# One layer of a hybrid RWKV-7 / S5 decoder: S5's merge for both token halves from one weight load and ahead of the RWKV merge, the block inversion issued step by step, and half-array low-rank products

## The chip, the cores and the metric

The program runs on one core of one Trainium2 chip, as a single launch over 1024 tokens of width 1024 in float32. The metric is device time in microseconds (us) from launch to end. The engines are named as in the profile: PE (TensorE) multiplies matrices, PEld is its weight load, DVE (VectorE) and ACT (ScalarE) do elementwise work, POOL (GpSimd) does little but issue transfers, and SP (SyncE) issues most of them. A difference of about half a per cent is what a measurement of this kernel can tell from none.

## The reference

```python
h = rms_norm(x, norm_mix_pre)
proj = h @ w_in                       # r,k,v, three low-rank downs | S5 input u | two gates
o_rwkv = rwkv7_branch(p_rwkv, ...) @ w_branch_rwkv
o_s5   = s5_branch(u_s5, ...) @ w_branch_s5
mixed  = (g_rwkv * o_rwkv + g_s5 * o_s5) @ w_out
x = x + rms_norm(mixed, norm_mix_post)
x = x + rms_norm(conv_ffn(rms_norm(x, norm_ffn_pre), ...), norm_ffn_post)

# inside rwkv7_branch (decay, in-context rate and gate are low-rank, ranks 64, 64 and 128)
w = -softplus(-(w0 + tanh(wd) @ w2)) - 0.5
a = sigmoid(a0 + ad @ a2)
g = sigmoid(gd) @ g2
# inside s5_branch
y = gelu(Re(C s) + D u)
return y * sigmoid(y @ w_glu + b_glu)
```

The RWKV state is carried through 1024 tokens, 8 heads of 64; the S5 state is a diagonal complex recurrence, 32 groups of 64 states. Everything else is dense products.

## The kernel before, in words

**Products.** Activations lie transposed: 128 channels on the partitions, tokens along the row, and the 1024 tokens are cut into two halves of 512, called `th` 0 and 1. Every float32 operand is split into a rounded high part (`hh`, `wh`: an ACT copy, lines 156 and 226) and the rest (`hl`, `wl`: a DVE subtract, lines 157 and 227). `mm3_steps` (lines 172 to 174) multiplies high by high, high by low and low by high: three matmuls of 128x128 by 128x512 for each 128 rows of the contraction. `load_w` fetches a weight tile of 128x512 and splits it. A tile's results collect in a PSUM buffer `gm` and are then evicted by ACT or DVE.

**Order.** The PE's order of instructions is the order in which the program issues them. `drive` in turn advances *lanes* (generators for the S5 scan, for its tables, for RWKV's preparation, chain and output), and between their steps the *fill*: a list of generators of dense products. A lane's `yield (cost, wait)` says what its step costs the PE in planned microseconds and how long the next step is to be held back; in the meantime fill is issued, and `PACE` says how much fill has to be issued per unit of lane work. The constants `T_...` are those waits. They do not make a chip wait: they only decide what stands ahead of what in the order. On DVE and ACT the order is made from priorities and planned readiness; `high_priority(HPW)` puts an instruction ahead of others that are ready.

**Stages of the first half of the program.** First `start` normalises and projects S5's input. Then the S5 stage runs the scan of four batches with `mix_in` as fill: the projections of r, k, v (`rkv`) and the low-rank products (`lowrank`), whose right-hand sides come from input-projection tiles 12 and 13. Then comes RWKV for half 0 and half 1. For each half:

1. `rwkv_front` builds the masked Gram blocks `gr` (lines 660 to 731);
2. `rwkv_inv` inverts the 32x32 diagonal blocks by 30 elimination steps of two DVE instructions each (lines 795 and 797), between two transposes (784, 798) and copies in and out of `gr` (`diagonal`, line 773);
3. `rwkv_level` joins 32-blocks to 64-blocks (line 812 transposes on DVE, 822 and 832 multiply on the PE);
4. `rwkv_chain` runs 8 chunks, each with three short PE steps that wait for ACT and DVE in turn (lines 879 to 904);
5. `rwkv_out` normalises each head, adds the bonus and applies the gate (lines 918 to 951).

The fill beside it is `rkv(2)`, `rkv(3)`, then 16 tiles of gates (`gate_tiles`, evicted at line 1158), then, once half 0 is out, `merge` (half 0: RWKV branch times gate, S5's GLU, S5 branch times gate, sum), `merge_s5` (half 1: GLU and S5 branch) and `outproj(0)`. After RWKV is done, `merge_rk` and `outproj(1)` finish half 1, and the feed-forward part follows, which takes the second half of the span and is not touched.

In the merges, `s5_y` (line 1178) loads the S5 output and applies gelu, `glu_tile` multiplies by `w_glu` and evicts at line 1188, `gate` multiplies by a branch weight and evicts on DVE at line 1203, line 1249 adds the two branches and lines 231 and 232 split the half-scaled sum. Both halves of S5's part load all 12 of its weight tiles (4 of `w_glu`, 8 of `w_br`), each half for itself.

**Low-rank products.** The two rank-64 products (decay and in-context rate) use a weight tile of 128 rows of which 64 are zeros, and one common right-hand side: 2 products by 2 halves by 4 tiles by 3 matmuls.

Of the kernel before, what the change touches and what calls it, by code (L numbers as in the profile page):

```python
# [66 lines left out]
class Kern:  # L67
# [425 lines left out]
    def s5_tables(self, b, d):  # L493
# [70 lines left out]
        for t, f in ((ph, s["fh"]), (sn, s["fl"])):  # L564
            for g in range(8):
                A.activation(t[:, g], self.cst("nrow"), AF.Identity, scale=f[:, b * 8 + g:b * 8 + g + 1])
        V.tensor_scalar(cs, ph, MAGIC, -MAGIC, ALU.add, ALU.add)
# [72 lines left out]
    def rwkv_front(self, d, g, th, pt, start):  # L640
# [122 lines left out]
    def diagonal(self, ds, m, back):  # L763
# [3 lines left out]
        for g, d in enumerate(ds):  # L767
            for blk in range(2):
                for h in range(2):
                    o, q = 64 * h + 32 * blk, 32 * (2 * g + blk)  # L770
                    x = d["gr"][o:o + 32, :, :, h, 32 * blk:32 * blk + 32].rearrange("p u c t -> p (u c) t")
                    y = m[q:q + 32, :, h]
                    (self.nc.scalar.copy if n % 2 else self.nc.vector.tensor_copy)(*((x, y) if back else (y, x)))
                    n += 1

    def rwkv_inv(self, ds, th):
# [5 lines left out]
        with self.tc.high_priority(HPW):  # L782
            self.diagonal(ds, x, False)
# [5 lines left out]
        yield 2.0, 0  # L789
        with self.tc.high_priority(HPW):  # L790
            for q in range(1, 31):
                m = 31 - q
                tm = self.tg("tm", 1, (128, 256), pool=self.rka)
                tv = tm[:, :q * m].rearrange("p (s t) -> p s t", t=m)
                V.tensor_tensor(tv, x2[:, 0:q, q:q + 1].to_broadcast([128, q, m]),
                                m2[:, q:q + 1, q + 1:32].to_broadcast([128, q, m]), ALU.mult)
                V.tensor_tensor(x2[:, 0:q, q + 1:32], x2[:, 0:q, q + 1:32], tv, ALU.add)
            V.transpose(mt.rearrange("p (e t) -> p t e", t=32), x.rearrange("p (q t) -> p t q", t=32))
            self.diagonal(ds, mt, True)

    def rwkv_level(self, ds):
# [13 lines left out]
        yield 0.4, T_LT  # L815
# [45 lines left out]
    def rwkv_chain(self, ds, pt, th):  # L861
# [7 lines left out]
        for c in range(8):  # L869
            z = self.z.pop(c)  # L870
            if th and not self.fac and len(self.ys5) == 4:
# [39 lines left out]
    def rwkv_out(self, ds, th, latency):  # L911
# [3 lines left out]
        for g in range(2):  # L915
# [12 lines left out]
            V.tensor_tensor(yn, yn, y.unsqueeze(2).to_broadcast([128, 16, 64]), ALU.mult)  # L928
        yield 0, latency
        for g, d in enumerate(ds):  # L930
            for u in range(2):
                p = 2 * g + u
                ps = self.rp((128, 4, 128))
                for c in range(4):
                    nc.tensor.transpose(ps[:, c], self.yn[:, g, c, u], self.cst("ident"))
                y1 = self.tg("ld", NLD)
                A.activation(y1, ps.rearrange("p c t -> p (c t)"), AF.Identity, bias=self.vec("lnx_b", p),
                             scale=self.vec("lnx_w", p))
                for src, op in ((d["bv"][u], ALU.add), (self.TG[p][:, o], ALU.mult)):
                    if th:  # L940
                        t = self.fac.pop(0)
                    else:
                        t = self.tg("ld", NLD)
                        nc.sync.dma_start(t, src)
                    V.tensor_tensor(y1, y1, t, op)
# [8 lines left out]
    def inproj(self, *jobs):  # L954

        ws = [self.load_w(self.a["w_in"][mt]) for mt, _ in jobs]
        for th in range(2):
# [133 lines left out]
    def shifted_into(self, xs, mt):  # L1091
# [3 lines left out]
        def use(th, ps):  # L1095
            y = self.shifted(ps, mt, th)
            if mt == 12:
                nc.scalar.activation(y[0:64], y[0:64], AF.Tanh)
            else:
# [5 lines left out]

    def lowrank(self, xs, js):

        nc = self.nc
        for j, hb, dst in js:
            w = self.load_w(self.a["w_lr"][j])  # L1110
            for th in range(2):
                for p in range(4):
# [3 lines left out]
                    if hb is None:  # L1116
                        nc.scalar.copy(t, ps)
                    else:
                        nc.scalar.activation(t, ps, AF.Tanh, bias=self.hb[hb][:, p:p + 1], scale=0.5)
                    if dst is self.TZ:  # L1120
                        nc.scalar.activation(t, t, AF.Identity, bias=self.ones1, scale=1.0)
# [11 lines left out]
    def mix_in(self):  # L1133

        def mixed(a, b, n):

            for i, c in enumerate(a):
                yield c
                if i % n == n - 1:
# [5 lines left out]
        xs = [[], []]  # L1145
# [3 lines left out]
        yield from mixed(self.rkv(1), self.lowrank(xs[1], ((2, None, self.TG),)), 4)  # L1149
# [4 lines left out]
    def gate_tiles(self, *ms):  # L1154
# [5 lines left out]
        yield from self.inproj(*((18 + m, lambda th, ps, m=m: use(m, th, ps)) for m in ms))  # L1160
# [14 lines left out]
    def s5_y(self, t, b, th, y):  # L1175

        self.nc.sync.dma_start(t, self.YU[b].rearrange("j c g n -> (c g) j n")[:, :, th * 64:th * 64 + 64])
        self.nc.scalar.activation(y.rearrange("p (n j) -> p j n", j=8), t, AF.Gelu_apprx_tanh)
        return y

    def glu_tile(self, m, xs, t, y, br, to):

        nc = self.nc
        w = self.load_w(self.a["w_glu"][m])
        ps = self.gmp()
        yield from self.mm3_steps(ps, w, 0, [x[0] for x in xs], [x[1] for x in xs])
        nc.scalar.activation(t, ps, AF.Tanh, bias=self.hb["b_glu"][:, m:m + 1], scale=0.5)
        nc.vector.scalar_tensor_tensor(t, t, 1.0, y(), ALU.add, ALU.mult)
        br.append(to())
        self.split_half(*br[-1], t)  # L1190
# [14 lines left out]
    def merge_load(self):  # L1205

        if self.outs >= 2 and not self.yr:
            for k in range(4):
                self.yr.append(self.tg("ld", NLD))
                self.nc.sync.dma_start(self.yr[k], self.YR[k])  # L1210

# [795 lines left out]
```

## Time and profile before

| | |
|---|---|
| median of three runs | 1464.04 us (1458.7 to 1464.59) |
| the profiled execution | 1461.26 us, its span 1459.5 us |
| PE busy | 1402.2 us, 96% of the span, 9156 matmuls |
| DVE busy | 1087.5 us, 75% |
| ACT busy | 746.7 us, 51% |
| mean granted PE clock | 0.986 |

A matmul's busy time in the profile is longer than the time after which the next one can start, since they overlap; so 96% is not the share of the PE's peak that is used. The windows view gives, for a stretch of the span, each engine's busy time (with the number of instructions), the granted PE clock, the DMA engines' busy share and the rate that they moved. The waits view names the waiting instruction, the one that it waited for, and then the total, the number of waits and the longest, in us.

### The profile page before, as it was taken

The page shows a single profiled execution, that of the slowest core. Times are in us where ns is not written, and L with a number is a line of the kernel's source. Part 1 is how long each engine was busy: PE and PEld are TensorE (multiplying, and loading weights), DVE is VectorE, ACT ScalarE, POOL GpSimd, SP SyncE. Part 2 cuts the span into 40 slices and gives each one's busy share as a digit, 9 for nine tenths or more (in the row PEclk, how much of TensorE's full clock was granted, in tenths as well). Part 3 has the DMA queues.
Part 4 walks back from the last instruction along what each step waited for, and adds up shares of the span by engine and source line. Part 5 has one row for each costly group of instructions (what it writes and reads, how often), then busy time and mean ns, then how long its engine had stood idle before and what let it go on. Part 6 is the DMA issues. An engine that isn't in the chain of part 4 may idle for free. (4 is left out here: it accounts for less than half of the span.)

```text
span 1459.5 us, 23887 instructions
## 1 busy us (share of the span) xinstructions
PE 1402.2 (96%) x9156; PEld 1142.9 (78%) x9156; DVE 1087.5 (75%) x1783; ACT 746.7 (51%) x1197; POOL 34.9 (2%) x80
## 2 busy tenths in 40 slices
PE   7999999999999989899999999999999999999996
PEld 5778888878878767678788887888888887888785
DVE  8986886378327788548688898777777777597677
ACT  7667775453424564535455464454544445444451
POOL 0000000000000000000000000000000000000001
PEclk9999999999999999899999999999999999999998
DMA  7454433542413565433555543222222228934723
GB/s 221 116 190 128 144 117 108 188 146 80 139 60 110 162 193 165 138 111 116 172 195 180 158 133 122 87 83 76 75 84 87 87 73 273 328 112 144 239 79 115
DMA packets 119682, 202.04 MB, mean 138 GB/s; under 512 B 28672, under 2 KB 34944, under 8 KB 119568
## 3 DMA queue, kind: packets, MB, share of 16 engines
q1 hardware_dynamic: 113296, 182.43, 39.4%
q0 software_dynamic: 4544, 15.80, 2.9%
q10 hardware_dynamic: 1728, 2.29, 0.4%
q8 instruction: 72, 1.18, 0.3%
q14 instruction: 42, 0.34, 0.1%
HBM read 148.04 MB, written 50.33 MB: 136 GB/s over the span
## 5 line engine op out<-in xcount | busy, mean ns | idle before, releaser
L172 PE MATMUL gm<-hh,wh 128*128 128x512 f32 x672 | 276.2, 411 | 9.1 <-DVE hl L1203 4.6
L173 PE MATMUL gm<-hl,wh 128*128 128x512 f32 x672 | 264.8, 394 | 0.0
L174 PE MATMUL gm<-hh,wl 128*128 128x512 f32 x672 | 264.6, 394 | 0.0
L156 ACT CAST wh<-wf 128x512 fp32r<-128x512 f32 x171 | 105.2, 618 | 140.9 <-PE gm L173 72.5
L157 DVE TENSOR_TENSOR wl<-wf,wh 128x512 fp32r<-128x512 f32 x171 | 117.2, 688 | 76.2 <-ACT wh L156 75.6
L172 PEld LDWEIGHTS gm<-hh,wh 128*128 128x128 f32 x672 | 127.5, 190 | 41.5 <-DVE hl L1203 5.7
L174 PEld LDWEIGHTS gm<-hh,wl 128*128 128x128 f32 x672 | 127.7, 190 | 27.8
L173 PEld LDWEIGHTS gm<-hl,wh 128*128 128x128 f32 x672 | 127.8, 190 | 24.7 <-issue 1.0
L1626 PE MATMUL d<-xl,wh 128*128 128x512 f32 x308 | 120.7, 392 | 2.1 <-DVE xl L227 2.0
L1625 PE MATMUL d<-xh,wh 128*128 128x512 f32 x308 | 120.8, 392 | 2.1 <-ACT xh L226 2.1
L1627 PE MATMUL d<-xh,wl 128*128 128x512 f32 x308 | 120.6, 392 | 0.0
L1451 PE MATMUL rp<-t,h 128*128 128x512 f32 x216 | 84.4, 391 | 1.5 <-ACT p L1465 1.5
L1453 PE MATMUL rp<-t,l 128*128 128x512 f32 x216 | 84.2, 390 | 0.5 <-DVE l L227 0.5
L1452 PE MATMUL rp<-t,h 128*128 128x512 f32 x216 | 84.1, 389 | 0.0
L1626 PEld LDWEIGHTS d<-xl,wh 128*128 128x128 f32 x308 | 58.2, 189 | 15.5 <-DVE xl L227 3.4
L1625 PEld LDWEIGHTS d<-xh,wh 128*128 128x128 f32 x308 | 58.2, 189 | 14.6 <-ACT xh L226 2.4
L1627 PEld LDWEIGHTS d<-xh,wl 128*128 128x128 f32 x308 | 58.1, 189 | 12.0
L226 ACT CAST h<-r 128x1024 fp32r<-128x1024 f32 x34 | 35.8, 1054 | 61.1 <-PE rp L1452 29.6
L227 DVE TENSOR_TENSOR l<-r,h 128x1024 fp32r<-128x1024 f32 x34 | 41.6, 1225 | 29.2 <-ACT h L226 27.7
L1472 DVE SCALAR_TENSOR_TENSOR y<-zv,vecs,y 128x1023 f32<-128x1023 f32 (+1 forms) x36 | 46.1, 1281 | 8.5 <-ACT y L1470 8.5
L1465 ACT COPY p<-rp 128x512 f32<-128x512 f32 x54 | 31.0, 574 | 36.6 <-PE rp L1453 36.6
L1451 PEld LDWEIGHTS rp<-t,h 128*128 128x128 f32 x216 | 40.5, 188 | 11.1 <-ACT p L1465 2.4
(459 smaller groups left out, 3127.6 us busy)
## 6 DMA issues: line engine op xcount, KB each, us to landing
r<-in_w_up_dram SPq DMA_DIRECT2D x36, 512.0 KB, 3.6
wf<-in_w_in_dram SPq DMA_DIRECT2D x62, 256.0 KB, 3.0
st<-in_w_down_dram SPq DMA_DIRECT2D x55, 256.0 KB, 4.0
st<-ACT SPq DMA_DIRECT2D x44, 256.0 KB, 4.3
wf<-in_w_up_dram SPq DMA_DIRECT2D x36, 256.0 KB, 2.9
ACT<-y POOLq DMA_DIRECT2D x18, 512.0 KB, 2.9
GT<-ev SPq DMA_DIRECT2D x32, 256.0 KB, 2.5
wf<-in_w_br_dram SPq DMA_DIRECT2D x32, 256.0 KB, 2.6
```

What stands on the lines that cost most here:

```text
L156: nc.scalar.copy(h[:, :n], f[:, :n])
L157: nc.vector.tensor_tensor(l[:, :n], f[:, :n], h[:, :n].bitcast(F32), ALU.subtract)
L172: mm(ps, a, xh[k], start=k == 0, stop=False)
L173: mm(ps, a, xl[k], start=False, stop=False)
L174: mm(ps, b, xh[k], start=False, stop=k == n - 1)
L1451: mm(ps, wh[:, c], xh, start=first and k == 0, stop=False, skip_group_check=True)
L1452: mm(ps, wh[:, c], xl, start=False, stop=False, skip_group_check=True)
L1453: mm(ps, wl[:, c], xh, start=False, stop=k == 3, skip_group_check=True)
L1472: V.scalar_tensor_tensor(y[:, lag:], z[:, 0:1024 - lag], self.vec(nme, i), y[:, lag:], ALU.mult, ALU.add)
L1625: mm(ps, wh[:, c], xh[:, x], start=start, stop=False, skip_group_check=True)
L1626: mm(ps, wh[:, c], xl[:, x], start=False, stop=False, skip_group_check=True)
L1627: mm(ps, wl[:, c], xh[:, x], start=False, stop=stop, skip_group_check=True)
```

## The change

The S5 part of the merge becomes one generator, `s5_unit`, for both halves: each of its 12 weight tiles is loaded once and used for both. It stands in the fill behind the last gate tiles and no longer depends on RWKV's half 0. Gelu moves beside the S5 scan: `s5_ready` applies it after each batch and stores the result in a new DRAM tensor `Y5`, from where `s5_unit` loads it. The merge of half 0 is what is left, `merge_rk0`; it and `outproj(0)` are all the fill that is added when half 0 is out. The last two gate tiles take half 1 first.

The inversion's 60 instructions are no longer issued in one go: after each step the lane yields until `begin + pace * q`, the pairs keep their order in the program on DVE, and the copies back are issued in four portions.

The two rank-64 products use 64-row slices for their third term: the high parts of both weights sit with the low parts of the same weight in one 128-row tile, so that one full matmul gives high by high and low by high, and a 64-row matmul gives high by low. They begin 12 steps into the projection of k, r, v.

Smaller edits: loads of RWKV's operands for half 0 go to POOL's queue, the factors of `rwkv_out` for half 0 are loaded a little earlier, the phase activations of the S5 tables are issued in four portions, and the planned waits and `PACE` have new values.

```diff
@@ rwkv_front
-            nc.sync.dma_start(t, src[:, o])
+            (nc.sync if th else nc.gpsimd).dma_start(t, src[:, o])
@@ rwkv_inv
+        begin, pace = self.now, T_Q2 if th else T_Q
+        for q in range(1, 31):
...
+            with self.tc.high_priority(HPW):
+                c = V.tensor_tensor(tv, x2[:, 0:q, q:q + 1].to_broadcast([128, q, m]),
+                                    m2[:, q:q + 1, q + 1:32].to_broadcast([128, q, m]), ALU.mult)
+                self.tc.keep_in_program_order(c)
+                c = V.tensor_tensor(x2[:, 0:q, q + 1:32], x2[:, 0:q, q + 1:32], tv, ALU.add)
+                self.tc.keep_in_program_order(c)
+            yield 0, begin + pace * q - self.now
@@ low-rank
+    def lowrank_pair(self, w, xs, js):
...
+                ps = [self.gmp() for a in range(2)]
+                for a in range(2):
+                    mm(ps[a], w[a][:, o], hi[a], start=True, stop=False)
+                for a, sl in enumerate(HALF):
+                    mm(ps[a], w[a][sl, o], lo[sl], start=False, stop=True)
+                yield 0.7
@@ mix_in
-        yield from mixed(self.rkv(0), self.lowrank(xs[0], ((0, "w0", self.TZ), (1, "a0", self.TA))), 3)
+        rkv = self.rkv(0)
+        yield next(rkv)
+        w = self.lowrank_w(js)
+        yield from mixed(rkv, self.lowrank_pair(w, xs[0], js), 4, 12)
@@ S5's merge
+    def s5_ready(self, b, tile=None):
+        for th in range(2):
+            t, y = tile(), tile()
+            self.nc.gpsimd.dma_start(...)      # YU[b] -> t
+            self.nc.scalar.activation(..., AF.Gelu_apprx_tanh)
+            self.nc.gpsimd.dma_start(self.Y5[b][:, th * 512:th * 512 + 512], y)
+    def s5_unit(self):
+        xs = [[self.halved(self.pair(1, 4 * th + b), self.Y5[b][:, o[th]]) for b in range(4)] for th in range(2)]
+        br = ([], [])
+        for m in range(4):
+            w = self.load_w(self.a["w_glu"][m])
+            for th in range(2):
...
+                nc.gpsimd.dma_start(y[1].bitcast(F32), self.Y5[m][:, o[th]])
+                yield from self.mm3_steps(ps, w, 0, [x[0] for x in xs[th]], [x[1] for x in xs[th]])
...
+        for m, th in [(m, th) for m in range(6) for th in range(2)] + [(6, 1), (7, 1), (6, 0), (7, 0)]:
+            if m not in ws:
+                ws[m] = self.load_w(self.a["w_br"][1, m])
...
+            yield from self.mm3_steps(ps, ws[m], 0, [x[0] for x in br[th]], [x[1] for x in br[th]])
+            nc.vector.scalar_tensor_tensor(f, t, 1.0, ps, ALU.add, ALU.mult)
+            if (m, th) == (7, 1):
+                self.yr_loads()
@@ the fill
-                self.fill = [self.mix_in()] + [self.gate_tiles(m) for m in range(14)] + [
-                    self.merge_loads(), self.gate_tiles(14, 15)]
+                self.fill = [self.mix_in()] + [self.gate_tiles(0)] + [self.s5_last()] + [self.gate_tiles(m) for m in range(1, 14)] + [
+                    self.gate_tiles(14, 15, order=(1, 0)), self.s5_unit()]
...
-                self.fill += [self.merge(mg), self.merge_s5(self.first), self.outproj(0, mg, self.mx0)]
+                self.fill += [self.merge_rk0(mg), self.outproj(0, mg, self.mx0)]
@@ planned waits
-T_LD, T_SQ, T_LT = 6.0, 3.0, 3.5
+T_LD, T_SQ, T_LT, T_LT2 = 12.86, 3.76, 4.74, 1.89
-T_LN, T_LE, T_INV2 = 32.0, 16.0, 46.0
+T_LN, T_LE, T_INV2 = 50.1, 14.13, 1.95
+T_Q, T_Q2 = 0.66, 1.2
+T_BACK, T_DIAG, T_PH = 3.0, 0.59, 0.41
-PACE, CREDIT = 0.8, 2.0
+PACE, CREDIT = 0.89, 2.0
```

More of the change, by code (lines that the diff above doesn't have):

```diff
@@ L935, in rwkv_out @@
                     nc.tensor.transpose(ps[:, c], self.yn[:, g, c, u], self.cst("ident"))
+                if not th:
+                    loads(p)
                 y1 = self.tg("ld", NLD)
@@ L1192, in gate_load, with yr_loads @@
+    def yr_loads(self):
+        if self.outs >= 2 and not self.yr:
+            self.yr = [self.halved(self.pair(0, 4 + k), self.YR[k]) for k in range(4)]
     def gate_load(self, j, m, th, t, eng=None):
@@ L1266, in slots @@
         return [self.early.tile([128, 512], F32R, tag=f"{n}{2 * k + i}", name=self.nm("e"), bufs=1) for i in range(2)]
-    def merge_s5(self, first):
-        br = []
-        for m in range(4):
-            yield from self.glu_tile(m, self.xs5, self.ev(), lambda: self.ys5[m], br, lambda: self.pair(0, 4 + m))
-        for m in range(NK):
-            first.append(self.hp[0].tile([128, 512], F32, tag=f"h{'lh'[m // 4]}{m % 4}", name=self.nm("hl"), bufs=1))
-            t = self.gate_load(1, m, 1, self.ev())
-            yield from self.gate(1, m, br, t, first[m])
     def rk_loads(self):
@@ L1809, in mix_out @@
         mg = []
-        self.fill += [self.merge_rk(self.first, mg), self.outproj(1, mg, mx)]
+        self.fill += [self.merge_rk(self.first[1], mg), self.outproj(1, mg, mx)]
         with self.tc.tile_pool(name="wfx", bufs=1, side="right") as self.wfp:
```

214 lines of the change are left out of this document (113 added, 101 removed).

## The prediction

> **What bounds the kernel now.** I read the page first, then windows along the span, then the PE's waits where it loses time, then who stands in front of the releasing instruction.
>
> From the page: the span, PE's and DVE's busy time.
>
> ```profile
> span 1459.5 us, 23887 instructions
> PE 1402.2 (96%) x9156; PEld 1142.9 (78%) x9156; DVE 1087.5 (75%) x1783; ACT 746.7 (51%) x1197; POOL 34.9 (2%) x80
> ```
>
> The PE is the bound, so time goes away only where a matmul goes away or an idle PE gets work. What one matmul costs is not its busy time of 0.39 us but the pitch. The PE's timeline in the S5 stage, first and last of 98 rows without a gap:
>
> ```profile
> 239.42 0.39 PE L173 MATMUL gm<-hl,wh 128*128 128x512 f32 x1
> ...
> 261.40 0.39 PE L174 MATMUL gm<-hh,wl 128*128 128x512 f32 x1
> ```
>
> (261.40 - 239.42) / 97 = 0.227 us. Windows (length, then PE, PEld, DVE, ACT, POOL busy, granted clock, DMA share, GB/s) show where the PE falls short of that:
>
> ```profile
> 75.00:100.00 25.00, 23.27 (x95) 18.99 (x96) 23.51 (x54) 17.59 (x31) 0.97 (x2) 0.93 0.53 181
> 100.00:250.00 150.00, 150.00 (x810) 126.44 (x810) 110.01 (x150) 106.77 (x192) 3.30 (x10) 1.00 0.43 130
> 250.00:400.00 150.00, 147.41 (x1331) 120.85 (x1333) 90.81 (x175) 66.24 (x135) 4.21 (x13) 1.00 0.41 138
> 475.00:600.00 125.00, 107.36 (x738) 85.44 (x739) 104.35 (x202) 73.35 (x137) 2.16 (x4) 0.93 0.57 176
> 600.00:665.00 65.00, 64.23 (x1268) 47.89 (x1267) 30.81 (x57) 25.41 (x55) 2.13 (x4) 0.98 0.33 105
> ```
>
> The stretch 475 to 600 is half 1's preparation. It is idle for 125 - 107.36 = 17.6 us, and its clock is 0.93, worth another 0.07 x 125 = 8.8 us: 26.4 us. Half 0's preparation (250 to 400) lost only 2.6 us at full clock, so the work itself doesn't force the loss. DVE is busy 83% there. The PE's waits of 475 to 600, with the two in 60 to 100 below:
>
> ```profile
> PE gm L172 <- DVE hl L1203: 4.6, 2, 3.9
> PE gm L172 <- DVE ev L1203: 3.1, 2, 2.2
> PE rp L822 <- DVE ld L812: 3.0, 1, 3.0
> PE cz L822 <- ACT hh L231: 2.2, 1, 2.2
> PE rp L701 <- ACT ld L937: 2.0, 1, 2.0
> PE rp L756 <- DVE ld L730: 1.7, 1, 1.7
> ...
> PE gm L172 <- ACT lx L226: 1.9, 1, 1.9
> PE gm L173 <- DVE lx L227: 0.5, 1, 0.5
> ```
>
> The first two, 7.7 us, are the merge: a PSUM buffer isn't evicted in time. The next two, 5.2 us, are `rwkv_level` behind late merge and transpose work. The last two of the six, 3.7 us, are `rwkv_front` and `rwkv_out`. DVE's work in the stretch, by line (count, busy, mean ns):
>
> ```profile
> L157 DVE TENSOR_TENSOR wl<-wf,wh 128x512 fp32r<-128x512 f32 x25 | 17.2, 688 | 1.3 <-ACT wh L156 1.2
> L795 DVE TENSOR_TENSOR tm<-mt 128x30 f32<-128x30 f32 (+14 forms) x30 | 10.0, 334 | 0.5
> L797 DVE TENSOR_TENSOR mt<-mt,tm 128x30 f32<-128x30 f32 (+14 forms) x30 | 10.0, 332 | 0.6
> L232 DVE SCALAR_TENSOR_TENSOR hl<-ev,hh 128x512 fp32r<-128x512 f32 x11 | 7.6, 691 | 1.5 <-ACT hh L231 1.2
> L227 DVE TENSOR_TENSOR hl<-ld,hh 128x512 fp32r<-128x512 f32 x8 | 5.6, 702 | 2.2 <-ACT hh L226 2.0
> L1203 DVE SCALAR_TENSOR_TENSOR hl<-ev,gm 128x512 f32<-128x512 f32 x8 | 5.4, 680 | 0.0
> ```
>
> So the inversion's 20 us and a merge with a DVE weight split for each 2.7 us of PE work (12 x 0.227) fall on the same stretch.
>
> **The change, part by part.** The sum is made against the profiled execution, 1461.3 us; the median of the runs, 1464.0, is 2.8 us above it.
>
> *Low-rank products, the wait.* They stood right behind tile 12's projection, whose result still had to pass ACT and DVE. Now 12 steps of 3 matmuls, 12 x 0.68 = 8.2 us, lie between, against a chain of a few 0.7 us operations. The 2.4 us of waits (1.9 + 0.5) go, and with them the clock of 0.93 in 75 to 100, 0.07 x 25 = 1.8 us. Together **-4 us**. If the cover were gone, 2.4 us come back.
>
> *Low-rank products, the count.* 2 x 2 x 4 x 3 = 48 matmuls, 48 x 0.227 = 10.9 us, become 16 full ones (3.6 us) and 8 pairs on half the rows. No such pair is in the trace; the nearest are the chain's 64x64 products, with full ones on both sides:
>
> ```profile
> 401.61 0.39 PE L174 MATMUL gm<-hh,wl 128*128 128x512 f32 x1
> 401.93 0.27 PE L887 MATMUL cz<-p,gr 64*64 64x64 f32 x2
> 401.94 0.27 PE L850 MATMUL cz<-V,gr 64*64 64x64 f32 x2
> ...
> 402.86 0.23 PE L859 MATMUL cz<-V,bk 64*64 64x64 f32 x2
> 403.02 0.50 PE L172 MATMUL gm<-hh,wh 128*128 128x512 f32 x1
> 403.36 0.39 PE L173 MATMUL gm<-hl,wh 128*128 128x512 f32 x1
> ```
>
> Two products on different halves start 0.01 us apart, so they run together; but the change of shape costs 0.32 - 0.227 = 0.09 us going in, about 0.14 coming out (0.16 to the next start, less a pair's own 0.02) and 0.34 - 0.227 = 0.11 on the first full one: 0.34 us a round. Together: 3.6 + 8 x (0.227 + 0.34) = 8.1 us, a gain of 2.8. One after the other: 3.6 + 8 x (0.454 + 0.34) = 10.0, a gain of 0.9. I take **-2.5 us**, nearer the row that runs together. The Trainium skill, "TensorEngine Tiling (Array Packing)", Theoretical Speedup, gives up to 2x for a contraction of 64 rows, which alone would make it 10.9 - 3.6 - 8 x 0.227 = 5.5 us; but its Key Properties say that a change of tiling mode drains the engine, and here the trace agrees and gives the drain its 0.34 us.
>
> *S5's merge.* No matmul is added or removed: 96 for the GLU and 192 for the branch, 288 x 0.227 = 65.4 us of PE work that is moved ahead of the RWKV merge. Removed are 12 weight loads: 12 x 0.69 = 8.3 us of DVE, the ACT copies beside them and 3 MB of transfers. Beside the inversion the fill is now GLU (0.69 + 4 x 0.69 = 3.4 us of DVE per 5.4 us of PE), then branch products (0.69 + 2 x 0.68 = 2.05 per 5.4). Before, the branch products of half 0 needed 0.69 + 0.68 + 0.69 + 0.69 = 2.75 per 2.7 us, all of DVE. That dense part remains for `merge_rk0`, but after the inversion and mostly in the chain, whose DVE was 30.8 us of 65. So most of the merge's 7.7 us should go; I take 6. Of the level's 5.2 us I take 2.5, since `merge_rk0` may still evict beside it. The 3.7 us in front and output I leave: the fill there stays gates, evicted by ACT.
>
> *The inversion step by step.* Its 20.0 us of DVE work are the same; what changes is what may stand between the steps. I give it no term of its own: it is what lets the evictions pass, counted above. Planned, it takes 30 x 1.2 + 3.0 + 3 x 0.59 + 1.95 = 42.7 us after the change, against 46.0 before. If it ended later, the level and the whole chain would start later (see the rivals).
>
> *The clock.* The dips stand behind the waits:
>
> ```profile
> 520.00:525.00 5.00, 3.35 (x27) 2.84 (x25) 4.97 (x13) 4.97 (x7) 0.91 (x2) 1.00 0.73 171
> 530.00:535.00 5.00, 1.79 (x6) 1.51 (x7) 3.66 (x10) 4.86 (x12) 0.00 (x0) 0.92 0.56 198
> 535.00:540.00 5.00, 5.00 (x18) 3.97 (x18) 3.68 (x8) 3.28 (x9) 0.00 (x0) 0.74 0.41 110
> ...
> 595.00:600.00 5.00, 2.47 (x64) 2.31 (x65) 2.69 (x4) 3.74 (x10) 0.00 (x0) 0.50 0.66 213
> ```
>
> A wait of 3.9 us is followed by 0.92 and 0.74, the level's waits by 0.50; the 1.65 us of idle in 520 to 525 stand at a clock of 1.00. With 8.5 of 17.6 us of idle gone I take the same share of the clock's 8.8 us, 4.2. Together **-12.7 us**. "TensorE: Matmul & The Clock Gate" of the Trainium skill, Part 1, has the clock halve after an idle window of about 3.4 us that runs freely; by it alone only the 3.9 us wait would surely cost clock, and the term would be nearer -9. The trace partly disagrees: waits of 2 to 3 us were followed by dips too.
>
> *What is added.* `s5_unit` overwrites half 1's projection inputs, so its 8 loads (2 MB on SP's queue, behind which later weight loads stand) can start only as half 1's last gate tile ends; 48 matmuls of half 0, 10.9 us, cover them. Loads from DRAM scratch land in
>
> ```profile
> ld<-YR SPq DMA_DIRECT2D x4, 256.0 KB, 4.4
> ev<-YU SPq DMA_DIRECT2D x4, 256.0 KB, 3.4
> ```
>
> 3.4 to 4.4 us, and four splits of 0.7 us follow on a busy DVE: near the cover's end if the queue is full. Without cover it is the whole 7 us; I take **+2 us**, between 0 and 7. Gelu beside the S5 scan costs ACT 8 x 1.2 us and some table loads, 6 to 8 by the alternation with sine:
>
> ```profile
> L1178 ACT ACTIVATE ld<-ev 128x512 f32<-128x512 f32 x4 | 4.7, 1184 | 2.7 <-DMA ev<-YU 2.7
> L573 ACT ACT_TABLE_LOAD x2 | 2.6, 1283 | 0.0
> ```
>
> Some 20 us at most on an ACT that is busy 107 of 150 us in 100 to 250, where the PE has no idle time: hidden, and 5 us at most if an eviction falls behind it in all four PSUM buffers. POOL's loads for half 0 and the 4 MB more of Y5 traffic lie in stretches with a DMA share of 0.4: nothing, 0 to 2 us.
>
> **Sum:** -4 - 2.5 - 12.7 + 2 = -17.2; 1461.3 - 17.2 = 1444.1. Runs lie up to 3 us above the profile, so I say **1445 us**. Its own range is 1434 (the front's and level's waits go too, with their clock) to 1454 (half of the 12.7 stays, added costs of 5).
>
> **The rivals.**
>
> *DVE stays the bound and the waits only move.* In 475 to 600 it loses 8.3 of 104 us at most and gets 5.5 us of S5 splits back; in-order, an eviction still stands behind inversion steps. For it: 83% busy now. Against: DVE had gaps, and the dense 2.75 per 2.7 us leaves. Then a third of the 12.7 stays as gain: 1461.3 - 4 - 2.5 - 4.2 + 2 = **1453**.
>
> *The fill runs dry behind the chain (slower).* Once `s5_unit` is done, only `merge_rk0` (96 matmuls, 21.8 us) and `outproj(0)` (192, 43.6 us) are left. Half 1's chain and output need cover:
>
> ```profile
> L904 DVE TENSOR_TENSOR S<-S,pt x8: 424/424/426, 613.1 to 662.4; 128x256 f32<-128x256 f32 x8
> ...
> L227 DVE TENSOR_TENSOR e<-ld,e x4: 684/692/694, 684.1 to 695.4; 128x512 fp32r<-128x512 f32 x4
> ...
> L172 PE MATMUL mm<-e,wh x32: 389/389/500, 709.9 to 770.4; 128*128 128x512 f32 x32
> ```
>
> The chain ends at 662.4 and the output's last split at 696; half 1's RWKV merge starts at 709.9. Beside the chain ran `merge_s5`, 144 matmuls or 32.7 us; behind it ran `outproj(0)`, 43.6 us, of which some 34 lay before that split. So about 67 us are wanted. Before, 76 us were left as the chain began; with the new order that is 76 plus or minus what the new pace and waits move. It decides when less than some 50 us are left then, `merge_rk0` mostly gone: a slower inversion or a larger `PACE` does that. With all of `merge_rk0` gone 67 - 44 = 23 us of idle come, and half-clock stretches of some 8 us by the rows above: 1444 + 31 = **1475**. Against: the planned inversion is 3 us shorter than before.
>
> *It does not do what it says:* the gates end later than I think, S5's part stands where the merge stood, and only the low-rank part counts, while the 2 MB burst costs its 7 us: **1461**.
>
> **How the numbers follow.** The forecast 0.62, DVE bound 0.18, fill dry 0.10, no effect 0.10. About 0.5%, 7 us, is what a measurement can tell here, so faster means under 1457: 0.62 x 0.95 + 0.18 x 0.75 = 0.72; same, 1457 to 1471, 0.17; slower 0.11. The range goes from 1430, where most of the 26.4 us are gained, to 1463: the dry case and a little at each end stay out.
>
> **What would show it.** 32 low-rank matmuls in place of 48, half-row pairs starting within some 0.02 us, and no wait on `lx`. In half 1's preparation fewer PE waits on line 1203's successors and a clock near 1. DVE weight splits down by 12 in all. A short wait at the first GLU product would show the burst; PE idle between the end of `outproj(0)` and the first `merge_rk` product the dry fill. I am wrong if half 1's preparation still loses over 20 us, or if a new gap over 5 us stands in the chain.

## The result

The changed kernel takes **1446.37 us** (median of four runs, 1445.47 to 1449.3) against 1463.16 us for the kernel before in runs beside it: a ratio of 0.9894, 95% interval 0.9867 to 0.992. The forecast was 1445 us. The profiled execution took 1445.47 us, 15.8 us less than the one of before, where the sum of the prediction had 17.2.

### The profile after

From the page of the changed kernel: span and busy time. 16 matmuls, 14 weight splits on DVE (157 instead of 171) and 7.9 us of PE busy time have gone (12 of the splits are S5's, two the low-rank products'), and the PE is still the bound.

```profile
span 1443.7 us, 23865 instructions
PE 1394.3 (97%) x9140; PEld 1134.2 (79%) x9140; DVE 1082.0 (75%) x1775; ACT 752.5 (52%) x1200; POOL 63.7 (4%) x124
```

The windows of the changed kernel, with the columns of the prediction (length, then PE, PEld, DVE, ACT, POOL busy, granted clock, DMA share, GB/s):

```profile
75.00:100.00 25.00, 22.69 (x93) 16.08 (x92) 23.93 (x52) 18.70 (x33) 0.98 (x2) 1.00 0.54 177
100.00:250.00 150.00, 147.75 (x794) 122.52 (x793) 106.10 (x145) 118.01 (x202) 11.46 (x21) 1.00 0.47 143
250.00:400.00 150.00, 145.55 (x1085) 119.62 (x1084) 94.27 (x175) 71.38 (x134) 20.50 (x38) 1.00 0.46 153
475.00:600.00 125.00, 118.74 (x1063) 95.08 (x1061) 104.96 (x215) 65.39 (x133) 6.48 (x12) 0.97 0.60 194
600.00:665.00 65.00, 64.52 (x1127) 48.71 (x1128) 43.11 (x78) 27.65 (x57) 2.13 (x4) 1.00 0.37 113
```

Half 1's preparation, 475 to 600, now idles 125 - 118.74 = 6.3 us instead of 17.6, and its clock of 0.97 costs 3.75 us instead of 8.8: the stretch loses 10 us where it lost 26.4. That is the forecast gain in the forecast place, 16.4 us for a predicted 12.7. But DVE is as busy there as before (104.96 us against 104.35), and two stretches became worse: 100 to 250 lost nothing before and now 2.25 us, 250 to 400 lost 2.6 and now 4.45.

The PE's waits of the changed kernel in 475 to 600 (instruction, what it waited for, total, count, longest):

```profile
PE gm L172 <- ACT ev L1269: 2.6, 2, 1.8
...
PE gm L172 <- DVE hl L1281: 0.7, 2, 0.5
```

The 7.7 us behind the merge's DVE evictions are 0.7 us (line 1281 is `gate`'s eviction now), the level's 5.2 us are 0.6, and the front's and output's 3.7, which I had left alone, are 2.2. The longest wait left is for ACT's eviction of a GLU tile (line 1269). DVE in that stretch, by line:

```profile
L157 DVE TENSOR_TENSOR wl<-wf,wh 128x512 fp32r<-128x512 f32 x15 | 10.3, 685 | 3.3 <-ACT wh L156 3.1
...
L1281 DVE SCALAR_TENSOR_TENSOR hl<-ev,gm 128x512 f32<-128x512 f32 x14 | 9.5, 682 | 0.5 <-PE gm L174 0.5
```

15 weight splits instead of 25, but 14 merge evictions instead of 8: more of the merge fits into the same stretch with the same DVE time. That is what the shared weight load should do there.

Two landmarks say when the gain is made. Rows of one line give the first and last start. Before, the last copy of the low-rank stage and the copies of `outproj(0)`:

```profile
L1117 ACT COPY ev<-gm x8: 568/578/588, 141.5 to 173.8; 128x512 f32<-128x512 f32 x8
L1327 ACT COPY mx<-gm x8: 576/579/587, 669.3 to 709.3; 128x512 f32<-128x512 f32 x8
```

The same in the changed kernel, with the chain's state update and the first product of half 1's RWKV merge:

```profile
L1177 ACT COPY ev<-gm x8: 561/582/592, 138.1 to 172.5; 128x512 f32<-128x512 f32 x8
L922 DVE TENSOR_TENSOR S<-S,pt x8: 424/424/427, 606.1 to 655.3; 128x256 f32<-128x256 f32 x8
L1369 ACT COPY mx<-gm x8: 576/579/586, 653.9 to 694.7; 128x512 f32<-128x512 f32 x8
L172 PE MATMUL mm<-e,wh x32: 389/389/500, 695.4 to 754.9; 128*128 128x512 f32 x32
```

The low-rank stage ends 1.3 us earlier, where the prediction had 6.5. `merge_rk` starts at 695.4 instead of 709.9, 14.5 us earlier, so 13.2 us are made between the two; the remaining 1.3 us come after it. The chain's last step stands at 655.3 instead of 662.4, and 0.7 us lie between the last copy of `outproj(0)` and `merge_rk`: the fill did not run dry.

### The profile page after: what moved, and what is told of

Its sections match the earlier page's. It is cut to its first block, busy times and chain, and to the rows that moved or that the text cites. A ratio compares the mean times of both kernels' runs of the same rounds, so it can differ in the third digit from the quotient of the medians.

```text
span 1443.7 us, 23865 instructions
## 1 busy us (share of the span) xinstructions
PE 1394.3 (97%) x9140; PEld 1134.2 (79%) x9140; DVE 1082.0 (75%) x1775; ACT 752.5 (52%) x1200; POOL 63.7 (4%) x124
## 5 line engine op out<-in xcount | busy, mean ns | idle before, releaser
L156 ACT CAST wh<-wf 128x512 fp32r<-128x512 f32 x157 | 96.8, 619 | 140.8 <-PE gm L173 77.0
L157 DVE TENSOR_TENSOR wl<-wf,wh 128x512 fp32r<-128x512 f32 x157 | 107.9, 689 | 79.6 <-ACT wh L156 78.1
L1667 PEld LDWEIGHTS d<-xh,wh 128*128 128x128 f32 x308 | 58.2, 189 | 14.5 <-ACT xh L226 2.5
```

What stands on the lines that cost most here:

```text
L156: nc.scalar.copy(h[:, :n], f[:, :n])
L157: nc.vector.tensor_tensor(l[:, :n], f[:, :n], h[:, :n].bitcast(F32), ALU.subtract)
L1667: mm(ps, wh[:, c], xh[:, x], start=start, stop=False, skip_group_check=True)
```

## The experiments

The main theory was the prediction's: one weight load for both halves and a merge ahead of `merge_rk0` unload DVE in half 1's preparation, and the stepwise inversion lets the evictions pass. Its rivals: the gain is the low-rank part, or the planned waits, which had no term. One form of the last rival stays open: the kernel before was not run with the new planned waits alone. Ratios are to the kernel before in runs beside each; the changed kernel's is 0.9894, and 0.9901 when it was run again among these.

### The changed kernel once more

> The changed kernel itself, beside the next three on one chip: a ratio of 0.989 to 0.990 to the kernel before, 1446 to 1448 us.

1447.49 us (1446.81 to 1448.08), ratio 0.9901 (0.9883 to 0.9919). The gain of about 1% stands on another chip too.

### S5's weights loaded for each half again

```diff
@@ s5_unit
         for m in range(4):
-            w = self.load_w(self.a["w_glu"][m])
             for th in range(2):
+                w = self.load_w(self.a["w_glu"][m])
...
-            if m not in ws:
-                ws[m] = self.load_w(self.a["w_br"][1, m])
+            ws[m] = self.load_w(self.a["w_br"][1, m])
```

> The changed kernel with each of S5's 12 weight tiles loaded and split once for each half, order unchanged: 8.3 us more on DVE, 7.4 on ACT, 3 MB more. If relief on DVE is what counts, PE waits of some 4 us come back: 1450. If order and position count, 1446 within 2 us.

1453.76 us (1452.11 to 1456.57), ratio 0.9946 (0.9927 to 0.9965): about 6 us lost. DVE's splits and the PE's waits of this kernel, first by line in 475 to 600, then in 600 to 665:

```profile
L157 DVE TENSOR_TENSOR wl<-wf,wh 128x512 fp32r<-128x512 f32 x28 | 19.2, 686 | 2.6 <-ACT wh L156 2.4
```

```profile
PE rp L850 <- ACT ld L844: 2.6, 2, 1.7
PE cz L850 <- ACT ld L844: 1.6, 1, 1.6
```

28 splits instead of 15, 8.9 us more. The PE's loss in 475 to 600 hardly moves (117.19 us busy at a clock of 0.99); what comes back is the wait of `rwkv_level`, a little later, with a clock of 0.95. So the shared load is worth some 6 us, but it is paid out at the level and the start of the chain, not at the merge's evictions where I had put most of it. That DVE's relief does it is not shown: the second loads also bring ACT copies and transfers, and the waits that came back are for an ACT copy (line 844).

### The inversion in one go again

```diff
@@ rwkv_inv
-        for q in range(1, 31):
...
-            yield 0, begin + pace * q - self.now
         with self.tc.high_priority(HPW):
+            for q in range(1, 31):
...
+            list(self.diagonal(ds, mt, True))
@@ planned waits: the same total, in one piece
-T_INV, T_INV2 = 2.61, 1.95
+T_INV, T_INV2 = 27.18, 42.72
```

> The changed kernel with each inversion issued in one go, at the same planned total (27.18 and 42.72 us). If single steps are what lets the merge's evictions pass on DVE, waits of the PE for S5's evictions come back in half 1's preparation, some 5 us with the clock: 1451. If the priorities interleave a block just as well (the trace of before shows splits and evictions between its steps), 1446 within 2 us.

1457.45 us (1453.78 to 1459.48), ratio 0.9968 (0.9954 to 0.9981): 10 us lost. Three views of this kernel: the PE's wait for the merge's eviction in 475 to 600; the only wait of 400 to 415; and two windows behind it:

```profile
PE gm L172 <- DVE hl L1269: 1.1, 2, 0.9
```

```profile
PE cz L838 <- issue: 2.4, 1, 2.4
```

```profile
405.00:410.00 5.00, 4.92 (x116) 4.47 (x116) 0.00 (x0) 2.90 (x8) 0.00 (x0) 0.56 0.02 5
410.00:415.00 5.00, 5.00 (x105) 3.57 (x105) 1.12 (x2) 0.99 (x2) 0.00 (x0) 0.76 0.01 3
```

The merge's eviction (line 1269 here) waits 1.1 us, and PE is busy 120.05 us of 125, no less than in the changed kernel. So the step of the prediction "it is what lets the evictions pass" is not what this shows. The 10 us are lost at other places: 250 to 400 (142.98 us busy against 145.55), 400 to 475, behind the pause of 2.4 us within half 0's level, after which the clock was 0.56 and 0.76, and half 1's chain (62.77 of 65 at 0.97). Of these, 400 to 475 costs 6 us (72.57 of 75 at 0.95, against 74.86 at 1.00), and the pause that stands there is not one of DVE or of an eviction (the last section comes back to it). So it is not shown that all of the 10 us are the inversion's own. The time lies beyond both expectations.

### The single steps alone, on the kernel before

The diff is the reverse of the one above, applied to the kernel before, with old waits; the planned total (34 and 46 us) is unchanged.

> The kernel before with the inversion issued step by step alone, at the same planned total. If single steps gain by themselves: 1456 to 1459, with fewer PE waits in 475 to 600. If they only pay together with S5's part beside them, as the prediction has it (no term of its own): 1462 within 3 us.

1467.66 us (1464.12 to 1470.83), ratio 1.0034 (1.002 to 1.0048): slower by 5 to 6 us. Its PE waits in 475 to 600:

```profile
PE gm L172 <- DVE ev L1219: 6.2, 1, 6.2
PE rp L701 <- ACT ld L953: 3.0, 1, 3.0
PE gm L172 <- DVE hl L1219: 2.8, 1, 2.8
```

With the old merge, the merge's evictions (line 1219 here) wait 9 us instead of 7.7. Single steps do not by themselves let evictions pass. But the stretch as a whole loses no more than before (107.07 us busy at 0.95, 24 us lost against 26.4), and the profiled execution, 1464.5 us, is only 3 us longer than the one of before: where the 5 to 6 us go is not shown. Neither expectation had a loss.

### S5's part alone, and with the single steps

The first is the kernel before with `s5_unit`, `s5_ready`, the order of the fill and the small load edits; low-rank, inversion, planned waits and `PACE` as before. The second adds the single steps. In both, the last gelu stands behind gate tile 5 (in the changed kernel it is tile 0).

```diff
-                self.fill = [self.mix_in()] + [self.gate_tiles(m) for m in range(14)] + [
-                    self.merge_loads(), self.gate_tiles(14, 15)]
+                self.fill = [self.mix_in()] + [self.gate_tiles(m) for m in range(6)] + [self.s5_last()] + [
+                    self.gate_tiles(m) for m in range(6, 14)] + [self.gate_tiles(14, 15, order=(1, 0)), self.s5_unit()]
...
-                self.fill += [self.merge(mg), self.merge_s5(self.first), self.outproj(0, mg, self.mx0)]
+                self.fill += [self.merge_rk0(mg), self.outproj(0, mg, self.mx0)]
```

> The kernel before with S5's part changed alone (both halves from one weight load, ahead of the RWKV merge, gelu beside the scan; last gelu behind gate tile 5; the small load edits), old low-rank products, old inversion, all planned waits and PACE old. If S5's part carries the gain by itself, as the prediction's terms have it (-12.7 + 2): 1451 to 1453 beside a before of 1462. If it only pays with the rest (the changed kernel with the inversion in one go lost 10 of 15 us): 1457 to 1463.

1466.57 us (1464.32 to 1475.37), ratio 1.0035 (1.0016 to 1.0054). No gain at all. The first three PE waits of 475 to 600:

```profile
PE gm L172 <- ACT ev L1252: 3.4, 3, 1.8
PE gm L172 <- DVE hl L1264: 3.2, 2, 3.0
PE rp L945 <- ACT V L763: 2.5, 1, 2.5
```

The stretch is better than before (110.48 us busy at 0.99, so 15.8 us lost instead of 26.4) and the next one worse (60.40 of 65 at 0.95, 7.9 us lost instead of 2.1): the waits moved from the merge to the output transposes of half 0 (line 945) and to the level. So S5's part alone does gain 10.6 us in the predicted place, and loses them elsewhere. A second loss stands in 400 to 475, where the kernel before lost nothing:

```profile
400.00:475.00 75.00, 74.17 (x1305) 56.27 (x1306) 17.97 (x41) 27.38 (x57) 0.30 (x4) 0.92 0.17 58
```

0.8 us idle and 6.0 us of clock, behind a pause of 2.9 us that ends at 400.8 and that the waits view puts down to no engine and no transfer (last section). Nothing ties this pause to the planned waits, so this run alone doesn't show that they are what S5's part lacked.

> The same with the inversion issued step by step at the same planned total; low-rank products and planned waits old. With the kernel before, before with steps alone (+6 us) and S5 alone this closes a square. If steps and S5's part help each other: at least 5 us below S5 alone. If the steps act alike with and without S5's part: 4 to 8 us above S5 alone.

1468.51 us (1464.5 to 1473.42), ratio 1.0038 (1.0021 to 1.0055). One wait in 475 to 600 alone is

```profile
PE rp L957 <- ACT bk L752: 6.4, 1, 6.4
```

the output transpose behind a copy of half 1's preparation. Neither edit of the pair, nor both, gains under the old waits. The square has neither of the expected forms: the steps cost 5 to 6 us on the kernel before and some 2, within the noise, beside S5's part.

### The old planned waits in the changed kernel

```diff
-T_LD, T_SQ, T_LT, T_LT2 = 12.86, 3.76, 4.74, 1.89
+T_LD, T_SQ, T_LT, T_LT2 = 6.0, 3.0, 3.5, 3.5
-T_KN, T_BK, T_GR, T_NF, T_MT, T_INV, T_LV, T_CH = 7.0, 5.1, 2.34, 5.0, 3.0, 2.61, 1.06, 0.8
-T_LN, T_LE, T_INV2 = 50.1, 14.13, 1.95
+T_KN, T_BK, T_GR, T_NF, T_MT, T_INV, T_LV, T_CH = 7.0, 4.0, 4.0, 5.0, 3.0, 9.43, 1.0, 0.8
+T_LN, T_LE, T_INV2 = 32.0, 16.0, 5.23
-T_N0, T_RS, T_N1, T_N2, T_N4, T_N5, T_N3 = 1.63, 3.58, 3.05, 4.43, 1.6, 37.27, 2.61
+T_N0, T_RS, T_N1, T_N2, T_N4, T_N5, T_N3 = 2.5, 4.0, 2.2, 5.0, 1.6, 40.0, 2.0
```

The inversion's old totals are kept, 34 and 46 us with the steps; `PACE` and the waits of the S5 scan stay new.

> The changed kernel with the planned waits of the RWKV stage and of the norms as before (PACE and the S5 stage's waits stay new, the inversion's planned total is the old one). The prediction gave the planned waits no term: then 1447 within 2 us. If the new values are a part of the gain, 1450 to 1458, with new PE waits in 250 to 475 or in the chains.

1464.49 us (1457.76 to 1467.17), ratio 1.0005 (0.9986 to 1.0025): **the whole gain is gone**, though every instruction of the change is there. The longest wait of 475 to 600, the longest of 600 to 665, and the two lines of the first of them (duration in ns, first and last start):

```profile
PE rp L703 <- ACT ld L961: 6.4, 1, 6.4
```

```profile
PE rp L850 <- ACT ld L844: 3.9, 1, 3.9
```

```profile
L703 PE MATMUL rp<-csts,gr x32: 270/273/475, 296.5 to 512.6; 128*128 128x128 f32 x32
L961 ACT ACTIVATE ld<-rp,vecs x8: 762/777/780, 511.1 to 696.8; 128x512 f32<-128x512 f32 x8
```

Line 703 belongs to half 1's front, line 961 evicts half 0's output transposes. `T_LN` is the planned wait ahead of those transposes. At 32 the first of these evictions starts at 511.1 us, before the front's last product at 512.6, which waits 6.4 us for it, with everything behind it in the order. At 50.1, in the changed kernel, the front is done at 508.7 and the first eviction starts at 525.2. So one cause of the loss is seen; the level's 3.9 us wait is a second. The second place costs more:

```profile
600.00:665.00 65.00, 59.16 (x1213) 44.11 (x1213) 33.78 (x62) 27.61 (x61) 0.00 (x0) 0.95 0.32 105
```

9.1 us are lost here against 0.5 in the changed kernel, and in 475 to 600 14.7 against 10.0. Which planned wait makes the level wait was not tried. The norms' waits can be worth little: they act behind RWKV, and from the first product of `merge_rk`, here at 706.6, to the end of the span it takes 749.6 us, against 748.3 in the changed kernel. The profiled execution (1458.02 us) is at the low end of these runs, so it shows more than 10 us of the loss, not all. The time lies beyond both expectations.

The kernel before has the same wait of its front for the output's eviction, only shorter: `PE rp L701 <- ACT ld L937`, 2.0 us, among the waits that the prediction shows. So a part of what the new waits bring might be had without any of the new instructions; no run tests that.

### More fill per unit of lane work

The dry-fill rival, provoked: `PACE` from 0.89 to 1.2.

> The changed kernel with PACE 1.2 in place of 0.89: more fill is issued per lane step, so less is left when half 1's chain begins. If the dry fill is real, its output stage shows PE idle between the end of the first output projection and the first product of half 1's RWKV merge, some 10 to 30 us, and the time is 1457 to 1475. If enough fill is left at any pace, 1447 within 4 us.

1475.38 us (1472.14 to 1478.64), ratio 1.0087 (1.0063 to 1.0111). Its window behind the end of the chain (last state update at 693.2 us) and of `outproj(0)`:

```profile
710.00:720.00 10.00, 0.90 (x7) 0.43 (x5) 7.53 (x13) 4.86 (x8) 0.00 (x0) 0.67 0.11 34
```

The last copy of `outproj(0)` is at 709.4, and of these 10 us the PE idles 9.1, at the place where the prediction looked for it, with the clock at 0.67. Half 1's output is split from 715.1 to 716.9, so the chain sets most of the gap; its end is a late weight, since ACT gets the first one of `merge_rk` only at 720.4. Some 28 us are lost against the changed kernel, and not all of it is dry fill: 9.6 us are a wait for a weight between 250 and 300 us, 5.9 us one in the level.

### Low-rank: the old products, and the old products begun late

The first puts the 48 full products back behind tile 12. The second keeps them full but lets them begin 12 steps into the projection of k, r, v, as the change does:

```diff
-        w = self.lowrank_w(js)
-        yield from mixed(rkv, self.lowrank_pair(w, xs[0], js), 4, 12)
+        yield from mixed(rkv, self.lowrank(xs[0], js), 3, 12)
```

> The changed kernel with the old low-rank products: 48 full matmuls, right behind tile 12's projection. By the prediction's terms (wait 4 us, count 2.5 us) it should take 1446.4 + 6.5 = 1453 us. By the trace of the changed kernel, where new PSUM waits of 2.4 us and drains stand in the same stretch, the new form gains hardly anything and this takes 1447 to 1448.

1455.44 us (1451.87 to 1458.34), ratio 0.9954 (0.9938 to 0.9969).

> The changed kernel with the old 48 full matmuls, but begun 12 steps into the projection. If the half-array form is worth its 2.5 us, this takes 1449. If the PSUM waits that come from two buffers per step eat that, it takes 1445 to 1447, and the waits on line 1162's successor are gone from its trace.

1452.77 us (1450.16 to 1454.46), ratio 0.9936 (0.9919 to 0.9954). Both lose, 8 and 5 us, and the second fits neither of its expectations; that looks like the predicted 6.5, but the trace says otherwise. Full and late products are the faster ones at their own place: no wait over 0.3 us from 60 to 130, and the stage ends 4.2 us before that of the changed kernel. Rows of `e_full_late`, the last copy of the low-rank stage, then the PE's wait from 250 to 300, then the window that holds it (the next 5 us have a clock of 0.50):

```profile
L1171 ACT COPY ev<-gm x8: 568/586/592, 138.4 to 168.3; 128x512 f32<-128x512 f32 x8
```

```profile
PE gm L172 <- ACT ev L1214: 5.7, 2, 4.9
```

```profile
285.00:290.00 5.00, 1.83 (x6) 1.54 (x6) 1.83 (x4) 3.33 (x5) 3.33 (x8) 0.56 0.91 294
```

The lead is lost behind a gate eviction (line 1214) that stands on ACT behind the last gelu; in `e_old_lowrank` the same wait is 4.7 us. ACT's timeline of the changed kernel shows the same place:

```profile
286.07 1.28 ACT L1240 ACT_TABLE_LOAD   x1 [1.73 <-DMA ev<-YU]
287.36 1.12 ACT L1240 ACTIVATE ev<-ev 128x512 f32<-128x512 f32 x1
288.28 0.64 ACT L1217 ACTIVATE ev<-gm,hb_b_gate 128x512 f32<-128x512 f32 x1
```

ACT idles 1.73 us for the landing of YU, loads gelu's table, runs gelu, and only then evicts a gate tile. In the changed kernel that costs the PE 1.6 us, in `e_full_late`, where the gates are further on, 5.7.

Why the half-array products gained little is in the PE's and ACT's timelines of the changed kernel:

```profile
83.72 0.61 PE L1156 MATMUL gm<-lx,lw 128*128 128x512 f32 x2
84.27 0.50 PE L1158 MATMUL gm<-lo,lw 64*128 64x512 f32 x2
84.70 0.50 PE L172 MATMUL gm<-hh,wh 128*128 128x512 f32 x1
85.04 0.39 PE L173 MATMUL gm<-hl,wh 128*128 128x512 f32 x1
```

```profile
87.54 0.31 ACT L517 ACTIVATE sml<-sml 64x128 f32<-64x128 f32 x1 [1.03 <-DVE sml L513]
...
88.19 0.69 ACT L1162 ACTIVATE ev<-gm,hb_w 128x512 f32<-128x512 f32 x1
```

From 83.72 to 85.04 stand two full products, a pair and one more full one in 1.32 us; seven full ones would be 7 x 0.227 = 1.59. So a round without a wait gains 0.27 us (four of the eight are like this one), and eight of them would gain 2.2. But a step now takes two PSUM buffers at once, and its evictions (line 1162) stand on ACT behind a step of the S5 tables (line 517) that waits for DVE, 1.03 us here and 1.83 us at 92.4. The PE's waits of 60 to 130 in the changed kernel are

```profile
PE gm L1156 <- ACT ev L1162: 2.4, 3, 1.5
PE gm L1156 <- DVE ev L1103: 0.5, 1, 0.5
```

2.9 us, more than the 2.2 that the fewer products gain. That the two buffers per step bring these waits is argued from the timeline; no run takes them away alone.

### The last gelu later, alone and with full late products

```diff
-                self.fill = [self.mix_in()] + [self.gate_tiles(0)] + [self.s5_last()] + [self.gate_tiles(m) for m in range(1, 14)] + [
+                self.fill = [self.mix_in()] + [self.gate_tiles(m) for m in range(6)] + [self.s5_last()] + [self.gate_tiles(m) for m in range(6, 14)] + [
```

> The changed kernel with the gelu of the last S5 batch moved from behind gate tile 0 to behind gate tile 5. Theory: in ACT's order it stands behind the landing of YU and between two table loads, and gate evictions wait behind it; its 1.6 us PE wait near 289 and part of the 2.4 us near 276 go: 2 to 4 us less than the changed kernel. Rival: the stretch is bound by its DMA share of 0.8 to 1.0 and the waits stay: no difference.

1449.6 us (1447.71 to 1451.25), ratio 0.9915 (0.9896 to 0.9934): not faster. The eviction's wait is gone, but 250 to 300 now has

```profile
PE gm L174 <- DVE wl L157: 2.7, 1, 2.7
PE gm L172 <- ACT wh L156: 2.4, 1, 2.4
```

waits for weights, at a clock of 0.93.

> Old full-array low-rank products begun 12 steps late, and the last gelu behind gate tile 5. Theory: the half-array form gains nothing locally (its trace idles 3.4 us in 60 to 130, against 0.4 for the full form), and what the full form lost stood behind the last gelu near 285 (5.7 us): 1443 to 1446, as fast as the changed kernel or up to 3 us faster. Rival: the half-array form is worth its 2.5 us: slower than the kernel with only the gelu moved by that.

**1443.49 us** (1441.25 to 1444.78), ratio 0.9869 (0.9847 to 0.9891). On the same chip the changed kernel took 1446.81 to 1448.08, so this one, with full products begun late and the last gelu behind gate tile 5, is 4 us faster than the changed kernel and 18 us faster than the one before. Its PE waits from 250 to 400, the longest two:

```profile
PE rp L703 <- ACT gr L689: 2.2, 1, 2.2
PE gm L172 <- ACT ev L1214: 1.9, 2, 1.1
```

The 5.7 us wait of the full late products is down to 1.9, and most of their lead is kept: half 1's RWKV merge starts at 692.7 us here, at 700.6 in `e_full_late` and at 695.4 in the changed kernel.

Four runs now form a square. With the last gelu behind gate tile 0, the half-array pairs are 5 us faster than the full late products (1447.5 against 1452.8); behind gate tile 5 they are 6 us slower (1449.6 against 1443.5). So the sign of this part is decided at the meeting point near 285 us, not by the products.

## Why the prediction was right in its number, and where its reasons were not

**The place: right. The size: in part luck.** Half 1's preparation gave 16.4 us for 12.7 predicted, with waits and clock in about the predicted share (11.4 and 5.0 us; I had 8.5 and 4.2). The front's and output's waits, left at zero gain, fell too. But low-rank gave 1.3 us for 6.5, so one term was 3.7 us too small and another 5.2 too large; that the total came within 1.4 us of the sum is luck.

**"The inversion step by step: no term of its own; it is what lets the evictions pass": not shown.** Undoing it costs 10 us, but not at the merge's evictions, and some 6 of them behind a pause that may not be its own; adding it alone loses 5 to 6 us, with longer waits at those evictions.

**"S5's merge ... most of the merge's 7.7 us should go": the cause was incomplete.** With S5's part alone that stretch does lose 10.6 us less, so the place was right; but the whole gains nothing (1.0035), since other stretches give it back. The second load of the weights costs some 6 us, seen at the level, for which I had taken 2.5.

**The planned waits: the failed step.** They have no term in the sum; I named them only as the inversion's total (42.7 us against 46.0). With those of the RWKV stage and of the norms put back the ratio is 1.0005. So a term that I had put at nothing, without a reason, is worth some 15 us in this kernel: without it no gain is left. What the new waits do is seen in one place, where they keep half 0's output behind half 1's front (`T_LN` from 32 to 50.1); the larger loss, at the level and in the chain, has no single wait to its name. The parts don't add: undone one at a time, low-rank costs 8 us, the second weight load 6, the inversion 10 and the waits 15, together 39 of a gain of 16; and S5's part and the single steps, added without the new waits, are worth zero or less (the low-rank part was not added alone). Whether the new waits would gain on the kernel before without the new instructions stays open.

**Low-rank, the wait: half right.** The waits on `lx` and the clock of 0.93 in 75 to 100 went as said. **The count: right in itself,** 2.2 us for 2.5; the pairs ran together, at 0.09 us going in, some 0.2 coming out and 0.11 on the first full product behind them. The Trainium skill, "TensorEngine Tiling (Array Packing)", Key Properties, says that a change of mode drains the engine; these rows agree and give it a price. What the term missed is the step that takes two buffers, whose evictions stand in ACT's order behind a step that waits: 2.4 us of waits on ACT and 0.5 on DVE. Taken together: 1.3 us at the landmark for 6.5.

**The added costs.** The burst of Y5 loads shows no wait on the first GLU products' inputs, only 2.6 us behind ACT's evictions at 543 to 547 us. So the burst that the +2 stood for cost nothing that the trace shows, and that another wait came out near it is luck. "Hidden, and 5 us at most" for gelu: the last one isn't hidden, it costs 1.6 us here and 5.7 in `e_full_late`; the mechanism that I named (an eviction behind it) is the one that came.

**The rivals.** DVE did not stay the bound of the stretch, with no less work in it. The dry fill didn't come, and came with `PACE` at 1.2 in the place named. That nothing would change did come, but with the old waits.

**The clock.** The prediction took dips after waits of 2 to 3 us. Here a wait of 4.9 us was followed by 0.56 and 0.50, the pause of 2.4 us by 0.56, while the changed kernel's 2.4 us wait in 250 to 300 left that stretch at a clock of 1.00. The Trainium skill, "TensorE: Matmul & The Clock Gate", Part 1, has a window of about 3.4 us that runs freely, so that what counts is how a pause falls into it; by that, not even the 3.9 us wait was sure to hold a whole window, as the prediction took it. That long waits dip agrees; that 2.4 us can go either way is what these rows show, and a window alone would not lead one to expect the dip after the shorter ones.

## What to carry to other kernels

In a kernel whose order is planned ahead, the planned waits are part of the change: test each part both by taking it out of the finished version and by adding it alone, since the two can have opposite signs, and test the waits by themselves on the old kernel too, which was left out here. Before giving a step two buffers or putting one more activation on ACT, look at which evictions stand behind it and what it waits for itself. A stage that gets faster locally (the full late products) can lose more at the next meeting point; follow landmarks, not only the stage.

## What the runs showed of the hardware that was not expected

Within bursts of small products, the level's 32x32 above all, the PE sometimes pauses while it waits for nothing that the waits view names ("issue"): 2.4 us at about 405 us in `e_inv_block`, quoted above, and in `e_s5_alone`, waits of 400 to 475,

```profile
PE rp L828 <- issue: 2.9, 1, 2.9
```

In the kernel before the one in the level of half 0 is 0.3 us. Each of these two is followed by a lower clock (0.56 and 0.76; a mean of 0.92 over 400 to 475). The length differs from kernel to kernel with the same products.

The DMA records of the traces point to a cause. The program itself comes in packets of 16 KB on a queue that the profile calls `instruction`. One of them lies inside the pause of `e_inv_block`; the DMA view of 402.55 to 403.65 us has

```profile
q8 instruction: 1, 0.02, 5.8%
```

It ends at 403.63 us, and the PE goes on at 405.08, 1.45 us later. In the traces of all fourteen kernels there are 17 pauses on "issue" of 0.3 us or more, and every one ends 1.2 to 1.5 us after such a packet has ended. So the PE most likely waits there for its own instructions. No run varied this, so it is not shown; but it means that an edit can move such a pause, and some 6 us with it, without touching what it was meant to test.

A pair of 64x512 products on the two halves of the array starts 3 to 4 ns apart, and the pair with the change of shape takes 0.43 us to the next start, against 0.227 for a full product.
